# Sliding-window copy: two final stores of 64 rows each, with their fill split two and a half to one and a half between VectorE and ScalarE

## The chip, the cores and the metric

One core of a Trainium2 chip. The metric is the device time of one execution in microseconds (us). The time includes about 1.8 us outside the span that the profile shows (191.79 us for a span of 190.0).

## The reference

Input `x` is 16 x 64 x 64 x 64 float32 (batch, channel, row, column). The output has, for each of 15 x 15 window positions, the 8 x 8 window of all channels, at a stride of 4:

```
result[:, i, j] = x[:, :, 4*i : 4*i + 8, 4*j : 4*j + 8]      # 16 x 15 x 15 x 64 x 8 x 8
```

There is no arithmetic. The input has 16.8 MB, the output 58.98 MB; a row of the output (one batch, one position) is 64 x 8 x 8 x 4 = 16,384 bytes.

## The kernel before

The input is loaded once into `L`. An output tile `G` (four buffers in turn) has 128 rows of 16 KB, one in each partition. ScalarE (`act`) and VectorE (`dve`, and `shf`, a stream shuffle used as a copy) copy windows from `L` into `G`; GpSimd sends each tile by an indirect store that scatters its rows ("scatter" below). A crossed tile has windows that reach over the border of two row groups; 16 of its 128 rows have no place in the output and are skipped. Which half of the partitions they lie in is set by `turn`. In the code `B` is 16 (batches), `HQ` 4 (row groups), `NY` 2 (halves of the batches), `QP` 32 and `HP` 64 (partitions), `CL` 32 (half of the channels), `ST` 4 (the stride) and `NSLOT` 4 (window positions of a row group).

```python
    nxt = [min(p + 1, 31) for p in range(32)]
    ...
            turn = crossed % 2          # in unit(j, s): a crossed tile
            crossed += 1
            fill(g, turn, s, j, 0, HP, (act, act))
            fill(g, 1 - turn, s + 1, j, 0, HP, (shf, mix))
            scatter(g, (idx_hi, idx_lo)[turn], j, s)
```

What no scatter covers is written at the end from two plain tiles of 64 rows, each by four plain stores of 16 rows:

```python
    j = NW - 1
    tile_()
    for s in range(2):
        g = tile_()
        cols = slice(j * ST, j * ST + WS)
        for y in range(NY):
            d = slice(QP + y * QP, QP + (y + 1) * QP)
            for ch, copy in enumerate((act, dve)):
                f = slice(ch * HP + y * QP, ch * HP + (y + 1) * QP)
                copy(out=g[d, ch * CL : (ch + 1) * CL, :, :], in_=L[f, :, s * ST : s * ST + WS, cols])
        g_q = g.rearrange("p c r w -> p (c r w)")
        for q in range(HQ):
            free((nc.sync, nc.scalar)[s * q % 2].dma_start(out=o_q[q * NSLOT + s, j], in_=g_q[QP + q : QP + q + (B - 1) * HQ + 1 : HQ]))
```

## Time and profile before

| | before |
|---|---|
| time, median of the first three runs | 191.98 us (191.85 to 192.25) |
| busy: VectorE, ScalarE | 142.7, 139.2 us of 190.0 |
| plain stores: issues by SyncE, ScalarE | 6 and 2, 256 KB each |
| fill of a plain tile: ScalarE, VectorE | 3.8, 2.45 us |
| last packet ends, last completion lands | 188.56, 189.09 us |

A transfer has landed when its semaphore gets its last count. The last row is from the records of single packets in the trace, as are all times of packets below; the profile's views add packets up. The two engines that copy are both busy for three quarters of the span, yet neither bounds it. The line of shares by slice (tenths of the 16 DMA engines' time) and the one of packets are the first to read:

```profile
DMA  2999999999999999999999999999999999999984
DMA packets 11156, 75.81 MB, mean 399 GB/s; under 512 B 3456, under 2 KB 3456, under 8 KB 7552
```

Only the first slice and the last two leave room. The change acts in the last two.

### The profile page before, as it was taken

The page shows a single profiled execution, that of the slowest core. Times are in us where ns is not written, and L with a number is a line of the kernel's source. Part 1 is how long each engine was busy: PE and PEld are TensorE (multiplying, and loading weights), DVE is VectorE, ACT ScalarE, POOL GpSimd, SP SyncE. Part 2 cuts the span into 40 slices and gives each one's busy share as a digit, 9 for nine tenths or more (in the row PEclk, how much of TensorE's full clock was granted, in tenths as well). Part 3 has the DMA queues.
Part 4 walks back from the last instruction along what each step waited for, and adds up shares of the span by engine and source line. Part 5 has one row for each costly group of instructions (what it writes and reads, how often), then busy time and mean ns, then how long its engine had stood idle before and what let it go on. Part 6 is the DMA issues. An engine that isn't in the chain of part 4 may idle for free.

```text
span 190.0 us, 556 instructions
## 1 busy us (share of the span) xinstructions
DVE 142.7 (75%) x200; ACT 139.2 (73%) x89; POOL 45.7 (24%) x50
## 2 busy tenths in 40 slices
DVE  4000007999998969899989999999999999995420
ACT  0000007999999979988889889999898699993750
POOL 7402203205635321422222222222222222222000
DMA  2999999999999999999999999999999999999984
GB/s 86 319 403 402 401 399 396 403 397 396 424 438 428 412 428 428 424 410 431 438 390 436 426 414 414 438 421 407 438 410 417 423 428 414 421 438 397 435 359 169
DMA packets 11156, 75.81 MB, mean 399 GB/s; under 512 B 3456, under 2 KB 3456, under 8 KB 7552
## 3 DMA queue, kind: packets, MB, share of 16 engines
q0 software_dynamic: 9040, 66.34, 84.8%
q1 hardware_dynamic: 2048, 8.91, 12.0%
q10 hardware_dynamic: 64, 0.52, 0.7%
q14 instruction: 4, 0.03, 0.0%
HBM read 16.78 MB, written 62.91 MB: 419 GB/s over the span
## 4 chain that ended last, share of the span: by engine, by line
DMA 54%; DVE 33%; issue 6%; POOL 2%; ACT 2%; DVEq 0%; PEldq 0%; ACTq 0%
DMA L<-in_x_dram 21%; DVE G L153 17%; DMA out_dram<-G,idx_hi 13%; DMA out_dram<-G,idx_y 13%; DVE G L146 11%; DMA out_dram<-G,idx 7%; DVE G L176 4%; POOL L L58 2%; ACT G L222 2%; DVE G L143 0%; POOL pi L69 0%; DVEq L153 0%; DVEq L176 0%; PEldq L256 0%; ACTq L222 0%
## 5 line engine op out<-in xcount | busy, mean ns | idle before, releaser
L143 ACT COPY G<-L 64x2048 f32<-64x2048 f32 x46 | 87.2, 1896 | 7.6 <-DMA out_dram<-G,idx 3.9
L176 DVE COPY G<-L 32x2048 f32<-32x2048 f32 x30 | 36.7, 1224 | 29.2 <-DMA L<-in_x_dram 26.1
L153 DVE STREAM_SHUFFLE G<-L 64x1024 f32<-64x1024 f32 (+3 forms) x40 | 55.6, 1391 | 1.3
L146 DVE STREAM_SHUFFLE G<-L 64x1024 f32<-64x1024 f32 x30 | 38.4, 1282 | 0.0
L176 ACT COPY G<-L 32x2048 f32<-32x2048 f32 x18 | 33.9, 1896 | 1.4 <-DMA out_dram<-G,idx_y 0.9
L176 ACT ACT_TABLE_LOAD x1 | 1.3, 1283 | 29.7 <-DMA L<-in_x_dram 29.7
L123 POOL DMA_INDIRECT out_dram<-G,idx_y x6 | 10.9, 1812 | 25.2 <-DVE G L176 15.6
L58 POOL DMA_DIRECT2D L<-in_x_dram x16 | 10.9, 696 | 24.3 <-DMA L<-in_x_dram 23.7
L123 POOL DMA_INDIRECT out_dram<-G,idx_hi x8 | 7.7, 962 | 30.6 <-DVE G L146 19.2
L123 POOL DMA_INDIRECT out_dram<-G,idx x8 | 9.1, 1136 | 19.9 <-ACT G L157 10.6
L123 POOL DMA_INDIRECT out_dram<-G,idx_lo x7 | 6.7, 962 | 27.4 <-DVE G L146 19.0
L222 ACT COPY G<-L 32x2048 f32<-32x2048 f32 x4 | 7.6, 1896 | 4.7 <-DMA out_dram<-G,idx_lo 3.5
L157 ACT COPY G<-L 64x256 f32<-64x256 f32 (+1 forms) x20 | 9.1, 456 | 0.5
L222 DVE COPY G<-L 32x2048 f32<-32x2048 f32 x4 | 4.9, 1220 | 4.9 <-DMA out_dram<-G,idx_hi 2.5
L143 DVE COPY G<-L 64x2048 f32<-64x2048 f32 x6 | 7.3, 1222 | 0.2
L153 DVE LOAD_MASK_SELECT G<-L x40 | 0.5, 12 | 2.1 <-DMA out_dram<-G,idx_y 0.9
L72 DVE TENSOR_SCALAR tb<-pi 128x1 int32<-128x1 int32 x1 | 0.2, 153 | 1.0 <-POOL pi L69 1.0
L78 DVE TENSOR_TENSOR th<-tc,tq 128x1 int32<-128x1 int32 x2 | 0.3, 156 | 0.0
L75 DVE TENSOR_SCALAR th<-tc 128x1 int32<-128x1 int32 x2 | 0.3, 154 | 0.0
L146 DVE LOAD_MASK_SELECT G<-L x30 | 0.2, 7 | 0.0
L69 POOL IOTA pi<- 128x1 int32 x1 | 0.1, 124 | 0.4 <-PEq L256 0.4
L78 DVE CUSTOM_DVE_ANT_0 idx_lo<-idx_lo,th 128x2 uint16<-128x2 uint16 x1 | 0.2, 160 | 0.0
(18 smaller groups left out, 2.6 us busy)
## 6 DMA issues: line engine op xcount, KB each, us to landing
L<-in_x_dram POOLq DMA_DIRECT2D x8, 1024.0 KB, 21.2
L<-in_x_dram SPq DMA_DIRECT2D x8, 896.0 KB
out_dram<-G SPq DMA_DIRECT2D x6, 256.0 KB
L<-in_x_dram POOLq DMA_DIRECT2D x8, 128.0 KB, 21.4
out_dram<-G ACTq DMA_DIRECT2D x2, 256.0 KB
out_dram<-G,idx POOLq DMA_INDIRECT x8, 13.7
out_dram<-G,idx_hi POOLq DMA_INDIRECT x8, 12.3
out_dram<-G,idx_lo POOLq DMA_INDIRECT x7, 11.4
```

What stands on the lines that cost most here:

```text
L58: eng.dma_start(out=L[p0 : p0 + QP - HQ + 1 : HQ, c0:c1, :, :], in_=x_v[ch, y, q, :, c0:c1, :])
L69: nc.gpsimd.iota(pi[:, :], pattern=[[0, 1]], base=0, channel_multiplier=1)
L72: nc.vector.tensor_scalar(out=d[:, :], in0=pi[:, :], scalar1=shift, scalar2=mask, op0=ALU.logical_shift_right, op1=ALU.bitwise_and)
L75: nc.vector.tensor_scalar(out=d[:, :], in0=a[:, :], scalar1=float(m), scalar2=None, op0=ALU.mult)
L78: nc.vector.tensor_tensor(out=d[:, :], in0=a[:, :], in1=b[:, :], op=op)
L123: st = nc.gpsimd.indirect_dma_start(out=o_v, out_offset=bass.IndirectOffsetOnAxis(ap=ix[:, 0:1], axis=0), in_=g.rearrange("p c r w -> p (c ...
L143: copy(out=g[d, cs, :, :], in_=L[f, :, s * ST : s * ST + WS, cols])
L146: nc.vector.stream_shuffle(out=g[d, cs, ST:WS, :], in_=L[f, :, 0:ST, cols], mask=nxt)
L153: nc.vector.stream_shuffle(out=out, in_=in_, mask=same)
L157: act(out=out[:, 0:k], in_=in_[:, 0:k])
L176: (act if (2 * d + ch) % 3 == 0 else dve)(out=g[d * QP : (d + 1) * QP, ch * CL : (ch + 1) * CL, :, :], in_=L[f : f + QP, :, s * ST : s * S ...
L222: copy(out=g[d, ch * CL : (ch + 1) * CL, :, :], in_=L[f, :, s * ST : s * ST + WS, cols])
```

## The change

The intent: fill the two plain tiles sooner, by giving half a block (1024 elements a partition) of ScalarE's share to the faster VectorE, and send each tile by one transfer instead of four.

```diff
+    half_c = CL // 2
     ...
-        for y in range(NY):
+        for y, ch, c0, c1, copy in (
+            (0, 0, 0, CL, act),
+            (0, 1, 0, CL, dve),
+            (1, 0, 0, half_c, act),
+            (1, 1, 0, CL, dve),
+            (1, 0, half_c, CL, dve),
+        ):
     ...     # the copy itself, with c0:c1 in place of the whole block
-        for q in range(HQ):
-            free((nc.sync, nc.scalar)[s * q % 2].dma_start(out=o_q[q * NSLOT + s, j], in_=g_q[QP + q : QP + q + (B - 1) * HQ + 1 : HQ]))
+        g_q = g.rearrange("p c r w -> p (c r w)")[QP : QP + B * HQ]
+        free((nc.sync, nc.scalar)[s].dma_start(out=o_q[s::NSLOT, j].rearrange("q b f -> b q f"), in_=g_q))
```

More of the change, by code (lines that the diff above doesn't have):

```diff
@@ L217 @@
         cols = slice(j * ST, j * ST + WS)
-        for y in range(NY):
-            d = slice(QP + y * QP, QP + (y + 1) * QP)
-            for ch, copy in enumerate((act, dve)):
-                f = slice(ch * HP + y * QP, ch * HP + (y + 1) * QP)
-                copy(out=g[d, ch * CL : (ch + 1) * CL, :, :], in_=L[f, :, s * ST : s * ST + WS, cols])
-        g_q = g.rearrange("p c r w -> p (c r w)")
-        for q in range(HQ):
-            free((nc.sync, nc.scalar)[s * q % 2].dma_start(out=o_q[q * NSLOT + s, j], in_=g_q[QP + q : QP + q + (B - 1) * HQ + 1 : HQ]))
+        for y, ch, c0, c1, copy in (
[5 more added lines that the diff above has]
+        ):
+            d = slice(QP + y * QP, QP + (y + 1) * QP)
+            f = slice(ch * HP + y * QP, ch * HP + (y + 1) * QP)
+            copy(
+                out=g[d, ch * CL + c0 : ch * CL + c1, :, :],
+                in_=L[f, c0:c1, s * ST : s * ST + WS, cols],
+            )
+        g_q = g.rearrange("p c r w -> p (c r w)")[QP : QP + B * HQ]
+        free((nc.sync, nc.scalar)[s].dma_start(out=o_q[s::NSLOT, j].rearrange("q b f -> b q f"), in_=g_q))
 _INS = ['x', 'window_size', 'stride']
```

## The prediction

> **What bounds the kernel now.** I read, in this order, the page's shares by slice, the busy times over three long stretches, the chain of waits from 168 us on, the groups of instructions and the order of instructions at the end, and last the DMA engines in the stretch where the change acts.
>
> The busy times over three stretches (the last three figures are the clock, the share of time in which the 16 DMA engines had a packet, and GB/s):
>
> ```profile
> 10.00:40.00 30.00, 10.09 (x9) 10.23 (x6) 5.38 (x7) 1.00 1.03 400
> 45.00:178.00 133.00, 122.94 (x166) 120.16 (x79) 34.04 (x29) 1.00 1.01 422
> 178.00:190.00 12.00, 2.44 (x2) 3.81 (x3) 0.00 (x0) 1.00 0.70 296
> ```
>
> Up to 178 us the DMA engines are never free (1.01 to 1.03) and move about 420 GB/s. Sixteen engines with 16,384-byte rows at 422 GB/s make 16 x 16,384 / 422e3 = 0.62 us a row: the unit of the rest. In the last 12 us the share is 0.70, so there the kernel looks like something else than DMA. The chain of waits says what, or seems to:
>
> ```profile
> 168.34 10.77 DMA out_dram<-G,idx_hi
> 179.11 0.02 issue
> 179.13 0.02 ACTq L222
> 179.15 0.04 issue
> 179.19 1.91 ACT G L222
> 181.09 0.01 issue
> 181.11 1.90 ACT G L222
> ```
>
> The second plain tile waits for its buffer (the scatter of 168.34 us lands at 179.11), ScalarE fills it in two copies until 183.01, and then the chain is silent, 7 us before the end of the span at 190.0. Those 7 us are the stores. The order of instructions shows both fills and the issues:
>
> ```profile
> 174.20 3.81 ACT L222 COPY G<-L 32x2048 f32<-32x2048 f32 x2 [3.52 <-DMA out_dram<-G,idx_lo]
> 174.24 2.45 DVE L222 COPY G<-L 32x2048 f32<-32x2048 f32 x2 [2.34 <-DMA out_dram<-G,idx_lo]
> 178.04 7.53 SPq L225 DMA_DIRECT2D out_dram<-G  x6
> 179.19 3.82 ACT L222 COPY G<-L 32x2048 f32<-32x2048 f32 x2 [1.17 <-DMA out_dram<-G,idx_hi]
> 179.20 2.47 DVE L222 COPY G<-L 32x2048 f32<-32x2048 f32 x2 [2.50 <-DMA out_dram<-G,idx_hi]
> 183.03 2.18 ACTq L225 DMA_DIRECT2D out_dram<-G  x2
> ```
>
> The reader is to see that ScalarE is 1.35 us behind VectorE in each fill, and that SyncE issues from 178.04 to 185.57. Both look like what sets the end. The view that decides is that of the DMA queues from 180.5 to 182.5 us (share of the 16 engines, each in use for one packet at a time):
>
> ```profile
> q0 software_dynamic: 26, 0.43, 50.0%
> q1 hardware_dynamic: 32, 0.26, 31.4%
> ```
>
> The scatter queue holds exactly half of the time of the 16 engines. I followed the packet records one by one: eight engines run out of scatter rows at 180.2, then take the plain store's rows as they come and stand idle between them, 1.6 to 2.0 us each. The other eight still have scatter rows until 183.2 to 184.3, take a first plain row shortly before those end and the others behind them, and go on without a gap. Five of them can be followed without doubt (a packet's record does not name its engine; I chained each row to the one that ended just before it): they end at 187.96 to 188.56 and stand idle 10 to 35 ns in all after 176 us. The last engine starts its eight rows of the last scatter at 178.76 and ends at 188.56: 8 scatter rows + 8 plain rows = 16 rows in 9.80 us, 0.6125 us each. **The bound of the end is one DMA engine that has work throughout**; the mean share of 0.70 hides it, as the other half of the engines wait. The rest of the end is 0.5 us until the last semaphore and 0.9 us of closing.
>
> **What the Trainium skill says.**
> - "DMA: Bandwidth & Descriptors", section "Why a DMA increments its semaphore by 16 and not by 1": the number of engines is the largest number up to 16 that divides the slowest dimension of both sides. Before it is 16 and 16 (16 rows); after, 64 partitions on the one side and 16 batches on the other, so again 16. The trace agrees for before: each plain store is 16 rows of 16 KB, one per engine.
> - The same page, "Issuing engines are not separate DMA queues": issuing from several engines saves only the sequencer's time. The trace agrees in that both hardware queues' rows stand behind each other on the same eight busy engines.
> - "ScalarE: Activation LUTs", section "What ACT_TABLE_LOAD costs": 186 ns + 0.833 ns an element, 1892 ns for 2048; the trace has 1896, and 616 for 512 where the rule says 612. So 1024 elements are estimated at 1.04 us.
> - "VectorE: DVE Perf Modes", "The perf-mode tier table": 1227 ns for a float32 copy of 2048 elements; the trace has 1220.
>
> **The change part by part.** The order of instructions is unchanged on every engine up to the last scatter; only the plain tiles differ.
>
> *The fill.* Removed: on ScalarE half a block (1024 elements) in each tile; added to VectorE: one copy of 1024. ScalarE: 1.90 + 1.04 = 2.94 us. VectorE: 1.22 + 1.22 + about 0.70 (half of the copy's 2048 elements, with some 0.15 us that do not shrink; an estimate from the page's rate, since no such copy is in the trace) = 3.14 us. The fill ends with VectorE after 3.14 instead of 3.81 us: 0.67 us earlier. The first store can be issued at 174.2 + 3.14 = 177.35 instead of 178.04, the second at 179.2 + 3.14 = 182.35 instead of 183.03. Does that shift the end? Those five engines reach the second tile's rows after 12 rows, the last at 178.76 + 12 x 0.6125 = 186.1, the earliest of them at 178.14 + 7.35 = 185.5. In before, the second tile's first rows begin 1.3 us after ScalarE's issue and 2.1 us after SyncE's; so after the change they are there by 182.35 + 2.1 = 184.5, 1.0 us before the first busy engine asks. They were there in time before, too (183.03 + 2.1 = 185.1). Worth on the path: 0.
>
> *The issues.* Six issues go: SyncE has one instead of six, ScalarE one instead of two. Consecutive issues of SyncE took 1.34 us each (the first 0.59). That is some 7 us less of sequencer time, all of it beside the busy engines' work: worth 0. A single transfer of 64 rows gives each engine 4 rows at once, so the eight waiting engines would lose their gaps and end earlier, perhaps by 186.9 instead of 187.2; they do not end last.
>
> *The bytes.* The same: 64 rows a store, 4 rows an engine, 16 rows left on the last engine. 178.76 + 16 x 0.6125 = 188.56, then 0.5 and 0.9: span 190.0 again. Eight completion writes an engine become two; the 0.6125 us between rows already include them and a packet itself takes 0.611 us, so six of them are at most 0.01 us.
>
> *Buffers.* The second tile's buffer is free when the scatter of 168.34 us lands. Rows of the first plain tile come 0.7 us earlier; could they delay that scatter's last rows? Its last rows end on the busy engines by 178.76; the new store's rows come at 177.35 + 1.3 = 178.65 at the earliest. At worst one engine takes one plain row ahead, 0.6 us later landing, which eats the gain of the fill but not the slack of 1.0 us.
>
> Sum: 0 (fill) + 0 (issues) - 0.01 (completions) = 191.98 - 0.01, about 191.9 us in round numbers, with a little credit for fewer semaphores to wait for at the close (nine waits of 0.06 us now, most of them passed before the last landing).
>
> **The rivals.**
> 1. *The fill sets the end*, as the chain of waits reads: the end moves with it, 0.67 us, 191.3 us. For it: the chain, and the share of 0.70 in the last 12 us. Against it: the gapless rows on five engines.
> 2. *The issues set the end*: the last issue begins at 184.40 now and would at 182.35, 2.05 us earlier, so 189.9 us (1.1% faster). For it: SyncE's issues of 1.34 us follow one another without a pause, and half of the engines do wait for them. Against it: the same rows; the waiting half ends 0.9 to 1.3 us before the last engine, so even they had slack.
> 3. *The large transfer runs on fewer engines*, split by its four row groups: 16 rows an engine, 16 x 0.61 = 9.8 us a store instead of 2.45 for each, some 10 us or more, about 202 us. For it: its outer side has a dimension of four. Against it: the instruction's dimensions are listed as 16 x 4 x 4096, the 16 outermost, and the rule of the skill gives 16. About 2%.
> 4. *The single long issue delivers late*: if 64 rows took four times the 1.34 us before the last row is there, 182.35 + 5.4 + 0.7 = 188.4, the end would barely move or come 1 us later. Against it: the loads of before have 224 rows an issue, and the first four issues took 0.68 to 0.87 us.
>
> **Range and chances.** The three runs of before span 191.85 to 192.25, so noise is 0.2 us each way. Rival 1 at full strength is 191.3; partial moves of rival 1 or 2 and the late variant give 191.4 to 192.4 as the range. Over 2% faster would need 188.1, which is more than even rival 2 gives: 0.01. Over 2% slower needs rival 3: 0.02. Within 2%: 0.97.
>
> **What would show each step.** Fill: ScalarE's part 2.94 and VectorE's 3.1 us, the stores' issues near 177.35 and 182.35. Issues: one each, under 1.5 us. Engines: in 180.5 to 182.5 the scatter queue's share falls below 50% while the sum of both queues rises towards 100%, since the free half no longer waits; the bytes still end near 188.5. The prediction is wrong if the last bytes end before 188.2: then the busy engines did have spare time or a faster row. It is wrong the other way if the landing of the scatter of 168.34 us moves past 180.1, or if the plain stores' rows show on fewer than 16 engines.

## The result, and the profile after

The changed kernel took 191.91 us (191.58 to 192.09, 6 runs), the kernel before in the same rounds and the earlier ones 191.75 us (191.56 to 192.25). The ratio is 1.0002, with a 95% interval of 0.9986 to 1.0017: the same. A ratio here is from runs of both kernels in the same rounds; it is not quite the ratio of the medians, nor of the means of all runs.

The changed kernel's order of instructions at the end:

```profile
174.14 2.96 ACT L228 COPY G<-L 32x2048 f32<-32x2048 f32 x2 [3.57 <-DMA out_dram<-G,idx_lo]
174.18 3.15 DVE L228 COPY G<-L 32x2048 f32<-32x2048 f32 x3 [2.40 <-DMA out_dram<-G,idx_lo]
177.41 0.65 SPq L233 DMA_DIRECT2D out_dram<-G  x1
179.16 2.96 ACT L228 COPY G<-L 32x2048 f32<-32x2048 f32 x2 [2.06 <-DMA out_dram<-G,idx_hi]
179.17 3.19 DVE L228 COPY G<-L 32x2048 f32<-32x2048 f32 x3 [1.84 <-DMA out_dram<-G,idx_hi]
182.45 0.64 ACTq L233 DMA_DIRECT2D out_dram<-G  x1
```

The fill is now nearly as long on both engines, the stores go out 0.6 us earlier, and the issue of 64 rows takes 0.65 us, where the first one of 16 took 0.59 and those behind it 1.17 to 1.37. All that was intended has happened. Still nothing came of it. The DMA queues of the changed kernel from 180.5 to 182.5 us:

```profile
q1 hardware_dynamic: 29, 0.48, 55.9%
q0 software_dynamic: 20, 0.33, 38.4%
```

Of the 16 engines' time 94.3% is used, instead of 81.4% before: the half of the engines that had run out of scatter rows now has plain rows without pauses in this stretch. (These engines pause once, by about 1 us, from 182.7 to 182.9 until the second tile's rows come at 183.8.) But look at what is left to do in the last us. First the kernel before, then the changed one (a stretch; then its length, the busy times of VectorE, ScalarE and GpSimd, the clock, the share of DMA time, GB/s; a packet appears to be counted in the stretch in which it starts):

```profile
185.20:186.20 1.00, 0.00 (x0) 0.00 (x0) 0.00 (x0) 1.00 0.70 295
186.20:187.20 1.00, 0.00 (x0) 0.00 (x0) 0.00 (x0) 1.00 0.85 361
187.20:188.20 1.00, 0.00 (x0) 0.00 (x0) 0.00 (x0) 1.00 0.36 148
```

```profile
185.20:186.20 1.00, 0.00 (x0) 0.00 (x0) 0.00 (x0) 1.00 0.73 311
186.20:187.20 1.00, 0.00 (x0) 0.00 (x0) 0.00 (x0) 1.00 0.58 246
187.20:188.20 1.00, 0.00 (x0) 0.00 (x0) 0.00 (x0) 1.00 0.35 147
```

From 186.2 to 187.2 less is moved than before, because the half that ends first is done by 186.4 instead of 187.2. From 187.2 to 188.2 the two kernels are alike: nine rows of 16 KB (147 KB), by the half that ends last. The last packet ends at 188.51 us (before: 188.56). Followed row by row, the eight engines of that half stand idle 10 ns at most in all after 176 us.

The page's line of packets has 11060 instead of 11156: 96 fewer, 6 stores by 16 completion writes, and the same 75.81 MB.

One thing was not foreseen: SyncE's last part. The view of what SyncE's queue waits for, before and after:

```profile
SPq L256 <- DMA out_dram<-G: 3.0, 2, 1.7
```

```profile
SPq L264 <- DMA out_dram<-G: 10.7, 2, 8.3
```

SyncE now has nothing to issue after 178.1 us and waits for the stores. From the last landing to the DRAIN instruction on SyncE that begins the close, 0.08 us pass before (189.09 to 189.17) and 0.45 us after (188.84 to 189.29). Why is settled by the ninth and tenth run.

### The profile page after: what moved, and what is told of

Its sections match the earlier page's. It is cut to its first block, busy times and chain, and to the rows that moved or that the text cites. A ratio compares the mean times of both kernels' runs of the same rounds, so it can differ in the third digit from the quotient of the medians.

```text
span 190.1 us, 551 instructions
## 1 busy us (share of the span) xinstructions
DVE 144.0 (76%) x202; ACT 137.5 (72%) x89; POOL 46.6 (24%) x50
## 2 busy tenths in 40 slices
DMA packets 11060, 75.81 MB, mean 399 GB/s; under 512 B 3360, under 2 KB 3360, under 8 KB 7456
## 4 chain that ended last, share of the span: by engine, by line
DMA 48%; DVE 38%; issue 7%; POOL 2%; DVEq 1%; PEldq 0%
DMA L<-in_x_dram 21%; DVE G L153 18%; DVE G L146 14%; DMA out_dram<-G,idx_hi 13%; DMA out_dram<-G,idx 8%; DMA out_dram<-G,idx_y 6%; DVE G L176 5%; POOL L L58 2%; DVE G L228 1%; DVEq L264 1%; DVE G L143 0%; DVEq L176 0%; POOL pi L69 0%; DVEq L153 0%; DVEq L228 0%
## 5 line engine op out<-in xcount | busy, mean ns | idle before, releaser
L176 DVE COPY G<-L 32x2048 f32<-32x2048 f32 x30 | 36.6, 1221 | 29.0 <-DMA L<-in_x_dram 26.1
L176 ACT COPY G<-L 32x2048 f32<-32x2048 f32 x18 | 33.9, 1896 | 1.2 <-DMA out_dram<-G,idx_y 0.8
L123 POOL DMA_INDIRECT out_dram<-G,idx x8 | 10.0, 1246 | 20.1 <-ACT G L157 10.6
L228 ACT COPY G<-L 32x2048 f32<-32x2048 f32 (+1 forms) x4 | 5.9, 1470 | 5.7 <-DMA out_dram<-G,idx_lo 3.6
L228 DVE COPY G<-L 32x2048 f32<-32x2048 f32 (+1 forms) x6 | 6.2, 1041 | 4.3 <-DMA out_dram<-G,idx_lo 2.4
```

What stands on the lines that cost most here:

```text
L123: st = nc.gpsimd.indirect_dma_start(out=o_v, out_offset=bass.IndirectOffsetOnAxis(ap=ix[:, 0:1], axis=0), in_=g.rearrange("p c r w -> p (c ...
L176: (act if (2 * d + ch) % 3 == 0 else dve)(out=g[d * QP : (d + 1) * QP, ch * CL : (ch + 1) * CL, :, :], in_=L[f : f + QP, :, s * ST : s * S ...
L228: copy(out=g[d, ch * CL + c0 : ch * CL + c1, :, :], in_=L[f, c0:c1, s * ST : s * ST + WS, cols],)
```

## The experiments

The theory: the end is set by the eight DMA engines that have rows without a pause, so the fill and the issues lie beside them. The rivals: the fill sets the end (rival 1), the issues do (rival 2), or the two parts of the change cancel. The expectations below call this last one rival 4; it is not the fourth rival of the prediction, a single issue that delivers late, which the profile after already rules out: its first row came 1.34 us after the issue, before any engine of the late half asked.

In the table, "rows" is the time from the issue of the last scatter until the last packet's end in the profiled execution. It takes out that whole executions run up to half a us early or late before the end. "Close" is the time from the last landing to SyncE's drain. The ratio is to the kernel before in the same rounds.

| run | time, us | ratio (95%) | rows, us | close, us |
|---|---|---|---|---|
| before (first trace) | 191.75 | 1 | 188.56 - 172.68 = 15.88 | 0.08 |
| changed kernel | 191.91 | 1.0002 (0.9986 to 1.0017) | 188.51 - 172.56 = 15.95 | 0.45 |
| e1_fill_alone | 191.45 | 0.9987 (0.9974 to 1.0001) | 188.61 - 172.66 = 15.95 | 0.08 |
| e2_store_alone | 191.71 | 1.0012 (0.9998 to 1.0026) | 188.05 - 172.18 = 15.87 | 0.45 |
| e3_slow_fill | 192.31 | 1.0040 (1.0027 to 1.0054) | 188.61 - 172.42 = 16.19 | 0.45 |
| e4_slower_fill | 194.39 | 1.0142 (1.0127 to 1.0158) | 191.24 - 172.89 = 18.35 | 0.45 |
| e7_eight | 194.50 | 1.0154 (1.0137 to 1.0170) | 191.31 - 172.65 = 18.66 | 0.38 |
| e8_half_row (wrong) | 190.82 | 0.9961 (0.9946 to 0.9977) | 187.38 - 172.70 = 14.68 | 0.45 |
| e5_turn | 190.74 | 0.9957 (0.9943 to 0.9972) | other order | 0.45 |
| e6_turn_before | 190.56 | 0.9940 (0.9927 to 0.9954) | other order | 0.08 |
| e9_again | 191.91 | 1.0006 (0.9993 to 1.0020) | 188.55 - 172.62 = 15.93 | 0.45 |
| e10_numbered | 190.93 | 0.9958 (0.9944 to 0.9971) | 187.88 - 172.89 = 14.99 | 0.08 |
| e11_turn_fill | 190.46 | 0.9928 (0.9915 to 0.9942) | other order | 0.08 |
| e12_turn_numbered | 189.81 | 0.9895 (0.9880 to 0.9910) | other order | 0.08 |

### Each part alone

`e1_fill_alone` is the changed kernel with the old stores:

```diff
-        free((nc.sync, nc.scalar)[s].dma_start(... one transfer of 64 rows ...))
+        for q in range(HQ):
+            free((nc.sync, nc.scalar)[s * q % 2].dma_start(... 16 rows, as before ...))
```

> Only the new split of the fill, with the eight stores of 16 rows as before. Theory (the end is set by the eight DMA engines that have rows throughout, so fill and issues lie beside them): the second fill ends 0.67 us earlier, the time of the kernel moves by less than 0.2 us (ratio 0.999 to 1.001), last packet again near 188.5. Rival 1, the fill sets the end: 0.67 us less, ratio 0.9965. Rival 4, two effects cancel in the whole change: this part alone gains 0.3 to 0.7 us and the other part alone loses as much.

Measured: 0.9987, 0.25 us less, with an interval from 0.50 us less to none. Rival 1's 0.9965 lies outside it. The rows took 15.95 us, no less than before's 15.88, so in the profiled execution the earlier fill did not bring the last row forward.

`e2_store_alone` is the kernel before with the new stores:

```diff
-        for q in range(HQ):
-            free((nc.sync, nc.scalar)[s * q % 2].dma_start(... 16 rows ...))
+        free((nc.sync, nc.scalar)[s].dma_start(... one transfer of 64 rows ...))
```

> Only the single stores of 64 rows, with the fill of one block pair per engine as before. Theory: under 0.2 us of change, ratio 0.999 to 1.001; the half of the engines that waits for rows ends near 187.0 instead of 187.2, the other half near 188.5. Rival 2, the issues set the end: 1.4 us less (the last issue begins at 183.0 instead of 184.4), ratio 0.993. Rival 4, cancelling parts: 0.3 to 0.7 us more.

Measured: 1.0012, 0.23 us more, with an interval from 0.04 us less to 0.50 more. Rival 2's 0.993 is far outside. So removing six issues gains nothing. The half that ends first was done by 186.5, earlier than the 187.0 expected. The rows took 15.87 us, as before, while the close took 0.37 us longer. That is a part of rival 4 that holds: the single stores cost a little, at a place apart from the stores' own time. Set side by side, the fill alone is worth 0.25 us less and the stores alone 0.23 us more, and neither is clear of 0. So the 1.0002 of both together may be nothing twice, or two small effects that cancel, a little below the 0.3 us that rival 4 was given at the least; more on this under "The close".

### How much slack the fill has

`e3_slow_fill` slows VectorE's part of the second tile's fill:

```diff
+            if s == 1 and copy is dve and c0 == 0:
+                copy = shf
```

> The changed kernel with VectorE's two whole blocks of the second plain tile by stream shuffle (2.43 us each) instead of copy (1.22 us): that fill takes 5.55 us instead of 3.15, so its store is issued near 184.75 instead of 182.45 and its rows are there by 186.1. Theory: in the changed kernel the busy engines begin the second tile's rows at 185.7 to 186.1, so the 2.4 us are nearly all slack: 0 to 0.4 us more. Rival 1, the fill sets the end: 2.4 us more, ratio 1.0125. Rival 2, the issues: 2.3 us more.

The issue came at 184.70, as planned. The ratio is 1.0040, or 0.77 us more than before (0.004 x 191.65), more than the 0 to 0.4 us expected; in the profiled execution the rows took 16.19 us, 0.24 more than in the changed kernel. That execution was the fastest of its five (192.03 us, median 192.31), so the trace shows less of the loss than the runs have. Either figure is far below rival 1's 2.4 us: two thirds or more of the delay was slack.

`e4_slower_fill` gives that fill to ScalarE alone:

```diff
+            if s == 1:
+                copy = act
```

> The changed kernel with all of the second plain tile's fill on ScalarE: 3 x 1.90 + 2 x 1.04 = 7.7 us, so its store is issued near 186.9 and its rows are there by 188.3. Theory: the slack of the previous run is used up, the busy engines wait: 188.3 + 4 x 0.6125 = 190.7 instead of 188.5, 2.2 us more, ratio 1.0115. Rival 1: 4.6 us more, ratio 1.024.

Now the slack is gone, and the DMA engines can be seen waiting. The order of instructions at the end of this run and its busy times (columns as above):

```profile
179.48 7.81 ACT L230 COPY G<-L 32x2048 f32<-32x2048 f32 x5 [2.02 <-DMA out_dram<-G,idx_hi]
187.32 0.64 ACTq L235 DMA_DIRECT2D out_dram<-G  x1
```

```profile
186.00:187.00 1.00, 0.00 (x0) 0.99 (x2) 0.00 (x0) 1.00 0.00 0
187.00:188.00 1.00, 0.00 (x0) 0.29 (x1) 0.00 (x0) 1.00 0.00 0
188.00:189.00 1.00, 0.00 (x0) 0.00 (x0) 0.00 (x0) 1.00 0.62 262
```

This is what a fill on the path looks like: two stretches in which no packet starts, then all 16 engines begin together, 1.3 us after the issue, and end together at 191.09 to 191.24. The rows took 2.40 us more than in the changed kernel (2.2 expected; the fill took 7.81 instead of 7.7 us); the time is 2.7 us above before. Rival 1's 4.6 us are excluded. In the changed kernel no such hole exists.

### The rows themselves

`e8_half_row` writes half of each row of the second plain tile (the result is wrong):

```diff
+        half = CFREE // (1 + s)
+        g_q = g.rearrange("p c r w -> p (c r w)")[QP : QP + B * HQ, 0:half]
     ...     # 0:half on the side of the output too
```

> The changed kernel with the second plain store writing only the first half of each row (a wrong result on purpose). Fill and issues as in the changed kernel. Theory: 4 rows of 8 KB instead of 16 KB on each engine, 4 x 0.31 = 1.2 us less, ratio 0.9937. Rivals 1 and 2: at most the last row's 0.3 us.

The rows took 14.68 us, 1.27 less than in the changed kernel; the time is 0.75 us below before (0.0039 x 191.65), which would be 1.1 us if the longer close of 0.37 us is taken out. Fill and issues were untouched, and their rivals had 0.3 us at most.

`e7_eight` sends that tile by two transfers of 32 rows, with 8 batches outermost:

```diff
     ...     # the first tile is sent by one transfer, as in the changed kernel
+        for y in range(NY):
+            free((nc.sync, nc.scalar)[y].dma_start(out=o_q[s::NSLOT, j, y * YB : (y + 1) * YB].rearrange("q b f -> b q f"),
+                 in_=g_q[QP + y * QP : QP + (y + 1) * QP]))
```

> The changed kernel with the second plain store cut by batches into two of 32 rows, whose outermost dimension is 8: by the rule of the skill such a transfer runs on 8 engines, so its 64 rows are 8 on each of eight engines and none on the others. Theory: if those eight are the half that ends last, 4 rows more each, 2.45 us more, ratio 1.0128; if they are the other half, these end at 183.8 + 8 x 0.6125 = 188.7 and the half that ended last at 186.1: 0.2 us more, ratio 1.001. Rivals 1 and 2: 0 (one issue more, on an engine of its own).

The first branch held: the eight engines that run such a transfer are those that ended last already. The Trainium skill's rule for the number of engines ("DMA: Bandwidth & Descriptors", section "Why a DMA increments its semaphore by 16 and not by 1") gives 8 here and 16 for the stores before and after, and the traces agree. Followed row by row, eight engines were done with everything by 182.9 us and the other eight went on until 190.7 to 191.3. The rows took 2.71 us more than in the changed kernel (four rows are 2.45; the other 0.3 us is one row on each of these engines, which started at about 186.9 and took 0.87 to 0.99 us instead of 0.61, why is not shown). The queues of this run from 186.5 to 190 us:

```profile
q10 hardware_dynamic: 23, 0.38, 25.1%
q1 hardware_dynamic: 24, 0.28, 23.2%
```

Together 48.3%: half of the engines, again behind an ordinary-looking mean.

### Moving rows from the half that ends last

If one half of the engines sets the end, giving some of its rows to the other half must gain. `e5_turn` does so by one digit:

```diff
-            turn = crossed % 2
+            turn = (crossed + 1) % 2
```

> The changed kernel with one character's worth of other order: the crossed tiles start with the other half, so of the 15 crossed scatters 7 skip 16 rows in partitions 64 to 127 and 8 skip 16 rows in partitions 0 to 63, instead of 8 and 7. The same bytes, fills and issues; two rows (2 x 0.6125 us) move from each engine of the half that ends last to each of the other half. Theory: the last half ends 1.2 us earlier, the other 1.2 us later (188.5 to 187.3, 186.3 to about 187), time 1.0 to 1.25 us less, ratio 0.9935 to 0.995. If the halves are assigned the other way round: 1.2 us more. Rivals 1 and 2 (fill, issues): 0.

0.9957, or 0.82 us less than before, and by the two ratios (0.9957 / 1.0002) 0.9 less than the changed kernel. The profile bears the mechanism out to the figure: the last packet ended at 187.34 instead of 188.51, 1.17 us earlier. The queues from 180.5 to 182.5 us now fill all of the engines' time (104%, as packets are counted whole), and in the last stretch there is nothing left:

```profile
q1 hardware_dynamic: 29, 0.48, 55.9%
q0 software_dynamic: 38, 0.41, 48.3%
```

```profile
186.20:187.20 1.00, 0.00 (x0) 0.00 (x0) 0.00 (x0) 1.00 0.24 98
187.20:188.20 1.00, 0.00 (x0) 0.00 (x0) 0.00 (x0) 1.00 0.00 0
```

All 16 engines end between 186.1 and 187.34. Against before the gain fell short of the 1.0 to 1.25 us expected. I had reckoned as if the changed kernel's close were that of the kernel before; with the 0.37 us of it, 1.2 becomes 0.83.

`e6_turn_before` is the same digit in the kernel before.

> The kernel before with the same other order of the crossed tiles. Theory: 1.0 to 1.25 us less than before, as the second tile's rows (184.3, 185.1, 185.9, 186.6 us by the four issues) come just in time for engines that ask from 184.3 to 184.9 on; at most 0.2 us worse than the changed kernel with that order. Rivals 1 and 2: 0 against before; and under them the changed kernel would stay as far from it as it is now.

0.9940, or 1.15 us less, as expected. But it was expected to be up to 0.2 us behind e5_turn and was ahead by 0.18 (medians 190.56 and 190.74): the close again, 0.08 against 0.45 us.

### The close

In the trace SyncE waits at the end for all DMA semaphores in order of their number, one wait every 0.06 us. The kernel before has 8 loads and 8 plain stores on 8 hardware semaphores, so that its last stores have the last numbers. In the changed kernel 8 loads are followed by 2 stores, which take the first two numbers; when the second store lands, the waits for the other six are still to be gone through. `e9_again` is the changed kernel unaltered, as a partner in the same rounds. `e10_numbered` makes 14 loads of the 8, so that the two stores get the last two numbers:

```diff
-                load(nc.sync, 0, y, q, SMALL, CL)
+                mid = SMALL + (CL - SMALL) // 2 if y * HQ + q >= 2 else SMALL
+                if mid > SMALL:
+                    load(nc.sync, 0, y, q, SMALL, mid)
+                load(nc.sync, 0, y, q, mid, CL)
```

> The changed kernel again, unaltered, as the partner of the next run on the same chip. Expected: ratio 1.000 to 1.002. In its trace SyncE runs through its nine closing waits in order of semaphore number; the second plain store has the third of them, so six more, 0.06 us each, follow its landing: 0.45 us from the last landing to the drain, as in the first trace (before: 0.08).

> The changed kernel with six of SyncE's eight loads cut in two, so that the two plain stores get the last two of the eight hardware semaphores instead of the first two; the bytes, packets, fills and stores stay. Theory (the rows set the last landing, and the single stores cost some time in the closing waits alone): 0.08 us instead of 0.45 from the last landing to the drain, 0.37 us less than the changed kernel, ratio 0.998 to 1.000 against before. If the single stores cost time elsewhere (on the engines): no gain over the changed kernel.

e9_again: 1.0006, and 0.45 us of close. e10_numbered: the close is 0.08 us, as expected. But the time fell by 0.98 us against e9_again, 0.6 more than the close explains. In the trace the last packet ends 0.67 us earlier (187.88 against 188.55), although the last scatter was issued 0.27 us later. The packet records put the start of this in the turn from loading to storing: 0.02 MB ahead of e9_again at 46 us, 0.15 MB at 80 us, 0.17 MB at 160 us (0.17 MB at 420 GB/s are 0.4 us). So the cut of the loads did something of its own that was not intended and that I cannot name; why the transfers run ahead from 46 us on stays open. For the close the run is clear, in the trace. What it is worth in time this run cannot say, but pairs of runs that differ in the stores alone can: before and e2_store_alone, e1_fill_alone and the changed kernel, e11_turn_fill (below) and e5_turn are 0.0012, 0.0015 and 0.0029 apart, with the single stores the slower by 0.2, 0.3 and 0.6 us, where the close makes 0.37. Pairs that differ in the fill alone (before and e1_fill_alone, e2_store_alone and the changed kernel, e6_turn_before and e11_turn_fill) are 0.0013, 0.0010 and 0.0012 apart, with the new fill the faster by about 0.2 us. Only e11_turn_fill and e5_turn have intervals that do not overlap, and four of the six pairs come from different rounds; but the signs agree. Where a gain of the fill would lie in the order of before, no trace shows.

e7_eight fits the order of the waits: with three plain stores the last one has the third number, one wait fewer is left behind it, and the close is 0.38 us.

### The best of it

> The other order of the crossed tiles, with the new fill and the eight stores of 16 rows. Theory: as the kernel before with that order (ratio 0.994), and up to 0.2 us less, since its second tile's rows, 0.67 us earlier, no longer come just in time: 0.993 to 0.994. If the fill were on the path: 0.9905.

> The changed kernel with both: the other order of the crossed tiles and the last two semaphores for the plain stores. Theory: 0.37 us less than the changed kernel with that order (0.9957): ratio 0.9938 to 0.9945, equal to the version with eight stores within 0.2 us. If the single stores cost time on the engines: 0.9957 again.

`e11_turn_fill` (the digit of e5_turn in e1_fill_alone): 0.9928, against 0.9940 for the same without the new fill. That is 0.2 us, as expected for a fill that no longer comes just in time, but the two intervals overlap. `e12_turn_numbered` (that digit in e10_numbered): 0.9895, 189.81 us against 191.78 for before and 191.91 for the changed kernel in the same rounds. It did better than expected (0.9938 to 0.9945), by about the share that the cut loads gave in e10_numbered. It is correct and beats both kernels by 1%.

## Why the prediction was right

- The bound: right. The last packet ended at 188.51 us, where 188.56 was predicted, on engines that stood idle 10 ns at most. Rows added (e7_eight), shortened (e8_half_row) and moved (e5_turn) shifted the last packet by 2.7, 1.3 and 1.2 us, close to the sizes that 0.6125 us a row gives.
- The fill: right. 2.96 and 3.15 us where 2.94 and 3.14 were predicted, issues at 177.41 and 182.45 where 177.35 and 182.35 were. Worth on the path: predicted 0; e1_fill_alone gives 0.25 us less with an interval that just reaches 0, so a small gain is not excluded. The slack was larger than the 1.0 us predicted: the second tile's rows were there from 183.79, and the first engine of the late half came to them at 185.68, 1.9 us later. e3_slow_fill used 2.25 us of delay and lost 0.24 us in the trace and 0.77 in the runs.
- The issues: right. 0.65 and 0.64 us, one each, and no gain (e2_store_alone).
- The engines: right that 16 are used, so rival 3 (fewer engines) did not come about. The half that ends first was done by 186.4, not 186.9: the second tile's rows came 1.34 us after ScalarE's issue (182.45 to 183.79), and I had allowed 2.1.
- The buffers: right. The scatter that the second tile waits for landed at 179.08 (before: 179.11). The first tile's rows did not start at 178.65, the earliest that was reckoned with, but at 180.25, after that landing.
- The completions: right, 96 packets fewer, of no weight.
- The close: wrong in sign. The sum of the prediction is 191.97; the rest down to its 191.9 is "a little credit for fewer semaphores to wait for at the close". The waits are as many as before and their order is by number; as the stores now have early numbers, the close is 0.37 us longer. The time did not show as much (1.0002 and 1.0006); what offsets it, a small gain of the fill or the last landing, which came 0.53 us after the last packet in the one trace of before and 0.33 to 0.35 in all others, is below what these runs resolve. That the time came out at 191.91, and not some 0.2 or 0.3 us higher, is to that extent luck.

## What to carry to other kernels

A mean DMA share of 0.7 at the end does not mean that DMA has ceased to be the bound: ask whether some of the engines have work without a pause, and compare what they have left with what the others have. Where they do, look there first: here an earlier fill gained some 0.2 us, not clear of the noise, and fewer issues nothing, while one digit that moved two rows an engine from one half to the other gained 0.8 to 1.15 us.

## What the Trainium skill lacked or had wrong

- "DMA: Bandwidth & Descriptors", section "Latency and other measured facts", gives about 600 ns to the first byte of a transfer from SyncE or ScalarE, and does not say from when. With all engines idle, e4_slower_fill has 1.3 us from the start of the issue to the first row (187.32 to 188.61), and 0.65 us from its end (187.96).
- No page that I found tells what a store's issue costs right behind another. SyncE's first of 16 rows took 0.59 us and the next three 1.35 to 1.37 us each; a single one of 64 rows took 0.65.
- "DMA: Bandwidth & Descriptors", section "Queues, rings and completion order", has an engine drain a packet, typically of some 9 to 17 descriptors, before it turns to the next queue. In the changed kernel an engine turned after each row: it took a scatter row and a plain row in turn, one of 16 KB each (182.24, 182.85, 183.47, 184.08 us).
- No page that I found has the close: the waits for all DMA semaphores in order of number, 0.06 us each, which put the end of them 0.08 or 0.45 us after the last landing as the last transfer has a late or an early number.
